# Second norm's last row block: the residual written into the accumulator banks, and the statistics read from them

## The chip, the cores and the metric

The kernel runs on one core of a Trainium2 chip. The engines named here are TensorE (PE in the profile, with its weight loads as PEld), VectorE (DVE), ScalarE (ACT), GpSimd (POOL) and SyncE (SP, which issues transfers). TensorE's results land in accumulator memory (PSUM); the kernel holds it as eight banks, each a tile of 128 partitions by 512 fp32 columns. The metric is device time in microseconds (us), the median of several executions; lower is better.

## The reference, cut to what matters

One decoder layer on 256 tokens of width 1024, batch 1. Only its last stage is touched:

```python
u = causal_dwconv(x @ w_up[l], conv_w_ffn[l])
f = (jax.nn.silu(u[..., :D_FF]) * u[..., D_FF:]) @ w_down[l]      # D_FF = 2816
x = layer_norm(DEEPNORM_ALPHA * x + f, ln2_g[l], ln2_b[l])        # over the 1024 columns
```

`layer_norm` takes mean and variance over the 1024 columns of a token, subtracts the mean, multiplies by 1/sqrt(variance + 1e-5) and by `ln2_g`, and adds `ln2_b`.

## The kernel before

Every fp32 operand of a product is split into a high and a low part (`h`, `l`), and each product is three matmuls (`mm3`: high by high, high by low, low by high), all added up in one bank. ScalarE makes the high parts of the weights (L196), VectorE the low ones (L205). The order of the work on each engine is written out by hand: an engine runs its instructions in the order in which the program issues them, and waits only where data or a buffer is not there. Those waits are put in from what each instruction reads and writes.

The down projection has 22 blocks (`NP`) of 128 rows of `w_down`. Its outputs are two row blocks of 128 tokens (`t` = 0 and 1) by two column halves (`nh`), in four banks: `dacc[t][nh]`. Blocks 0 to 13 go into all four banks inside the loop over the up projection's columns. The last eight blocks (`TAIL` = 8, blocks 14 to 21) go in a hand-written tail:

- L1012 to L1014: the eight blocks' products for row block 0, beside the last splits and the last pieces of the activation.
- L1029 to L1040: row block 0's norm on VectorE: `residual` (L797, and `bn_stats` in L799), `norm_stats` (`bn_aggr` in L781, the power -0.5 on GpSimd in L782), `norm_apply` (L786, L787) and two output transfers on SP's queue.
- Row block 1, on TensorE in this order: columns 0 to 511 of the eight blocks into `dacc[1][0]` (L1047), columns 512 to 767 into a fresh bank (e2, L1056), columns 768 to 1023 into another fresh bank (e3, L1062).
- Row block 1 on VectorE: the residual and what blocks 0 to 13 left in the banks are put into three SBUF pieces `part` (L1050), with their row sums. e2 is added to its piece (L1057). e3 is added last (L1076).

Row block 1's mean is known before its last columns are. ScalarE sums the `w_down` rows of blocks 14 to 21 over columns 768 to 1023 beside splitting them (`rowsum`, L199), scales the activations by these sums (`fs`, L1021), GpSimd adds the eight up (L1024), and TensorE multiplies the total by ones (`mean`, L1065): the sum over the last 256 columns of products that are not there yet. With the mean (L1068), ScalarE squares and sums the first 768 columns (L1071), VectorE subtracts the mean and multiplies by `ln2_g` (L1073, L1074), and behind the last bank VectorE adds it (L1076), squares and sums it (L1077), GpSimd takes the power -0.5 (L1079), and VectorE finishes in two pieces of 640 and 384 columns (L1082), each with its output transfer (L1083), the first on SP's queue and the second on ScalarE's.

Of the kernel before, what the change touches and what calls it, by code (L numbers as in the profile page):

```python
# [8 lines left out]
F32 = mybir.dt.float32  # L9
F32R = mybir.dt.float32r  # L10
BF16 = mybir.dt.bfloat16
I32 = mybir.dt.int32
AF = mybir.ActivationFunctionType
ALU = mybir.AluOpType

P = 128
S = 256
D = 1024
# [6 lines left out]
NP = DFF // P  # L25
ALPHA = 2.0 ** 0.25
EPS = 1e-5
# [22 lines left out]
CHUNK = 2048  # L50

PIECES = {0: (0, 768, 1280, 1792), 1: (0, 768, 1792)}
OFF_B, OFF_C, OFF_H, OFF_G = 3 * AW, 3 * AW + CW, 3 * AW + 2 * CW, 3 * AW + 3 * CW
TAIL = 8


def plan():
# [49 lines left out]
    for c in range(1, NP // 2):  # L107
# [4 lines left out]
        d = c - 1  # L112
        if 0 <= 2 * d < NP - TAIL:
            mark(("dn", d))
            rows("w_dn", 2 * d)
    for d in range((NP - TAIL) // 2, NP // 2):
        if ("dn", d) not in first:
# [20 lines left out]
def layer_kernel(ctx: ExitStack, tc: tile.TileContext, x, wpack, cpack, ln1_g, ln1_b, ln2_g, ln2_b, out):  # L138
    nc = tc.nc

    cst = ctx.enter_context(tc.tile_pool(name="cst", bufs=1))
    big = ctx.enter_context(tc.tile_pool(name="big", bufs=1))
    wp = ctx.enter_context(tc.tile_pool(name="wp", bufs=1))
    tmp = ctx.enter_context(tc.tile_pool(name="tmp", bufs=1))
# [11 lines left out]
    def scratch(shape, name, bufs=None, tag="scr"):  # L156
        return tmp.tile(shape, F32, tag=tag, name=name, bufs=bufs or 6)
# [4 lines left out]
    RAW_BUFS, HL_BUFS = 3, 9  # L162
    chunks, plan_units, U = plan()
# [13 lines left out]
                nc.sync.dma_start(xr, x[0].rearrange("(t p) d -> p t d", p=P))  # L177


    LAST_UNITS = [U[("dn", i // 2)] + i % 2 for i in range(NP - TAIL, NP)]  # L180
    rowsum = cst.tile([P, TAIL], F32, name="rowsum")

    def alloc(u, part, tag):
        k, n = units[u]["shape"]
# [7 lines left out]
    def split_h(u):  # L192

        issue_dma(units[u]["chunk"] + RAW_BUFS - 1)
        alloc(u, "h", "wh")
        nc.scalar.activation(units[u]["h"], raw_of(u), AF.Copy)  # L196
        if u in LAST_UNITS:
            j = LAST_UNITS.index(u)
            nc.scalar.activation(scratch([P, 256], f"rowsum{j}", tag="gs", bufs=3), raw_of(u)[:, 0, 768:1024], AF.Copy,  # L199
                                 accum_out=rowsum[:, j:j + 1])  # L200

    def split_l(u):

# [3 lines left out]
    def raw_of(u):  # L207
        un = units[u]
        k, n = un["shape"]
        return raws[un["chunk"]][:, un["off"]:un["off"] + k * n].rearrange("p (k n) -> p k n", k=k)  # L210
# [15 lines left out]
    def hl_split(h, l, src, eng=None):  # L226
        nc.scalar.activation(h, src, AF.Copy)  # L227
        (eng or nc.vector).tensor_tensor(l, src, h.bitcast(F32), op=ALU.subtract)  # L228
# [24 lines left out]
    neghalf = cst.tile([P, 1], F32, name="neghalf")  # L253
# [15 lines left out]
    xT = big.tile([P, KT, 2, S], F32R, tag="xT", name="xT")  # L269
# [43 lines left out]
    def mm3(o, ah, al, bh, bl, start, stop):  # L313

        nc.tensor.matmul(o, ah, bh, start=start, stop=False)  # L315
        nc.tensor.matmul(o, ah, bl, start=False, stop=False)  # L316
        nc.tensor.matmul(o, al, bh, start=False, stop=stop)  # L317
# [376 lines left out]
    for j in reversed(range(16)):  # L694
        u = U[("g", 0)] + j
# [26 lines left out]
    def ps_pair(name):  # L722
        return pairs.tile([P, 2, 512], F32, tag="pair", name=name)
# [65 lines left out]
    x1 = big.tile([P, 2, D], F32, tag="rows", name="x1")  # L789
    x1T = big.tile([P, KT, 2, S], F32R, tag="xT", name="x1T")  # L790

    def with_eps(stats):

        nc.vector.tensor_scalar(stats[:, 0, 2:3], stats[:, 0, 2:3], EPS * D, None, op0=ALU.add)
# [47 lines left out]
    ln2 = big.tile([P, 2, D], F32, tag="e8", name="ln2")  # L842
# [6 lines left out]
    def f_tile(i):  # L849
        g = i // 8  # L850
        if g not in FT:
            FT[g] = big.tile([P, 8, 2, S], F32R, tag=("b16", "c16", "b16")[g], name=f"f{g}")
        return FT[g][:, i % 8]
# [78 lines left out]
    dacc = [[acc_bank(f"d{t}{nh}") for nh in range(2)] for t in range(2)]  # L932

    def down(i, ts=(0, 1), nhs=(0, 1)):
        un = units[U[("dn", i // 2)] + i % 2]
        ft = f_tile(i)
        for t in ts:
            for nh in nhs:
                mm3(dacc[t][nh], ft[:, 0, t * P:(t + 1) * P], ft[:, 1, t * P:(t + 1) * P],
                    un["h"][:, 0, nh * 512:(nh + 1) * 512], un["l"][:, 0, nh * 512:(nh + 1) * 512],  # L940
                    i == 0, i == NP - 1 or (t == 1 and nh == 1 and i == NP - TAIL - 1))

    def down_part(i, bank, c):
        un = units[U[("dn", i // 2)] + i % 2]
        ft = f_tile(i)
        mm3(bank[:, 0:256], ft[:, 0, P:2 * P], ft[:, 1, P:2 * P],
            un["h"][:, 0, c * 256:(c + 1) * 256], un["l"][:, 0, c * 256:(c + 1) * 256], i == NP - TAIL, i == NP - 1)


    pending = []  # L950
# [11 lines left out]
    for c in range(1, NP // 2):  # L962
        for e in range(2):
            i = 2 * c + e
# [24 lines left out]
    for k, (kind, i, u) in enumerate(seq[:tail_from]):  # L989
        if kind == "g":  # L990
            pair, first_unit = ps_pair(f"pb{i}"), u
# [24 lines left out]

    fs = big.tile([P, TAIL, 2, P], F32, tag="d8", name="fs")
    for j in range(TAIL):  # L1020
        nc.scalar.activation(fs[:, j], f_tile(NP - TAIL + j)[:, :, P:2 * P].bitcast(F32), AF.Copy, scale=rowsum[:, j:j + 1])  # L1021

    def fs_add(a, b):
        nc.gpsimd.tensor_tensor(a, a, b, op=ALU.add)  # L1024

    fs_add(fs[:, 0:2], fs[:, 4:6])
    fs_add(fs[:, 2:4], fs[:, 6:8])

    r0 = x1[:, 0]  # L1029
    stats = tmp.tile([P, 4, 6], F32, tag="stats", name="rstats", bufs=2)  # L1030
    for nh in range(2):
        residual(0, nh, dacc[0][nh], x1, r0, stats, nh, nh * 512, nh * 512 + 512)
    mv = norm_stats(r0, stats, 2)
    fs_add(fs[:, 0:2], fs[:, 2:4])
    fs_add(fs[:, 0], fs[:, 1])
    fs_add(fs[:, 0, 0], fs[:, 0, 1])
    for c in range(2):
        cc = slice(c * 512, (c + 1) * 512)
        norm_apply(r0[:, cc], r0[:, cc], mv, ln2[:, 0, cc], ln2[:, 1, cc])
        nc.sync.dma_start(out[0, 0:P, cc], r0[:, cc])  # L1040


    cols3 = (slice(0, 512), slice(512, 768), slice(768, D))
    part = [scratch([P, cc.stop - cc.start], f"part{c}") for c, cc in enumerate(cols3)]
    sums = tmp.tile([P, 12], F32, tag="sums", name="sums", bufs=1)
    for i in range(NP - TAIL, NP):
        down(i, (1,), (0,))  # L1047
    for c in (1, 2, 0):
        bank = dacc[1][1][:, 256 * c - 256:256 * c] if c else dacc[1][0]
        nc.vector.scalar_tensor_tensor(part[c], x1[:, 1, cols3[c]], ALPHA, bank, op0=ALU.mult, op1=ALU.add,  # L1050
                                       accum_out=None if c == 1 else sums[:, c:c + 1])
    fsr = big.tile([P, 2, P], F32R, tag="xT", name="fsr")
    hl_split(fsr[:, 0], fsr[:, 1], fs[:, 0, 0])
    bank = ps_pair("e2")[:, 0]
    for i in range(NP - TAIL, NP):
        down_part(i, bank, 2)  # L1056
    nc.vector.scalar_tensor_tensor(part[1], bank[:, 0:256], 1.0, part[1], op0=ALU.mult, op1=ALU.add, accum_out=sums[:, 1:2])  # L1057
    nc.vector.tensor_reduce(sums[:, 3:4], sums[:, 0:3], axis=mybir.AxisListType.X, op=ALU.add)
    bank = ps_pair("e3")[:, 0]
    mean = acc_bank("mean")  # L1060
    for i in range(NP - TAIL, NP):
        down_part(i, bank, 3)  # L1062
        if i == NP - TAIL + 1:
            for part_hl in range(2):
                nc.tensor.matmul(mean[:, 0:2], fsr[:, part_hl], ones, start=part_hl == 0, stop=part_hl == 1)  # L1065

    for c, f in ((4, -1.0 / D), (5, -1.0 / (32 * D))):
        nc.vector.tensor_scalar(sums[:, c:c + 1], mean[:, 0:1], sums[:, 3:4], f, op0=ALU.add, op1=ALU.mult)  # L1068
    res = wp.tile([P, CHUNK], F32, tag="raw", name="res", bufs=RAW_BUFS)
    for c in range(2):  # L1070
        nc.scalar.activation(scratch([P, 512], f"sq{c}")[:, 0:cols3[c].stop - cols3[c].start], part[c], AF.Square,  # L1071
                             bias=sums[:, 5:6], scale=1.0 / 32, accum_out=sums[:, 6 + c:7 + c])
        nc.vector.scalar_tensor_tensor(res[:, cols3[c]], part[c], sums[:, 4:5], ln2[:, 0, cols3[c]], op0=ALU.add, op1=ALU.mult)  # L1073
    nc.vector.tensor_scalar(part[2], part[2], sums[:, 4:5], None, op0=ALU.add)  # L1074
    nc.vector.tensor_scalar(sums[:, 8:9], sums[:, 6:7], sums[:, 7:8], EPS, op0=ALU.add, op1=ALU.add)
    nc.vector.tensor_tensor(part[2], part[2], bank[:, 0:256], op=ALU.add)  # L1076
    nc.vector.tensor_tensor_reduce(out=scratch([P, 256], "sq2"), in0=part[2], in1=part[2], scale=1.0 / D, scalar=sums[:, 8:9],  # L1077
                                   op0=ALU.mult, op1=ALU.add, accum_out=sums[:, 9:10])
    nc.gpsimd.tensor_tensor(sums[:, 10:11], sums[:, 9:10], neghalf, op=ALU.pow)  # L1079
    nc.vector.scalar_tensor_tensor(res[:, cols3[2]], part[2], 1.0, ln2[:, 0, cols3[2]], op0=ALU.mult, op1=ALU.mult)  # L1080
    for cc, queue in ((slice(0, 640), nc.sync), (slice(640, D), nc.scalar)):
        nc.vector.scalar_tensor_tensor(res[:, cc], res[:, cc], sums[:, 10:11], ln2[:, 1, cc], op0=ALU.mult, op1=ALU.add)  # L1082
        queue.dma_start(out[0, P:2 * P, cc], res[:, cc])  # L1083


# [40 lines left out]
```

## Time and profile before

| what | value |
|---|---|
| median of 3 runs | 363.85 us (363.8 to 364.34) |
| the profiled execution | 364.61 us, of which the span shown by the profile is 362.8 us |
| mean granted TensorE clock | 0.995 |
| PE, PEld busy | 355.3 us, 307.0 us |
| DVE, ACT, POOL busy | 299.9 us, 235.4 us, 24.9 us |

The profile is of one execution. The "span" runs from its first to its last instruction. A timeline row gives the start from the beginning of the span, the duration, the engine, the line of the kernel, the operation, the tile it writes and those it reads, the count, and in brackets the idle time before it with whoever ended that. A group row gives the count, the total busy time, the mean in ns, and the idle time before. TensorE's matmuls overlap, so the distance between two starts, and not the duration, is what one matmul costs.

### The profile page before, as it was taken

To read this page: it belongs to the slowest core of one execution; us is meant where nothing else is said; L and a number is where in the kernel's file an instruction comes from. 1 tells how busy PE (TensorE), PEld (TensorE's weight loads), DVE (VectorE), ACT (ScalarE), POOL (GpSimd) and SP (SyncE) were. 2 spreads that over 40 slices of the span, in tenths; PEclk is the share of its full clock that TensorE was granted. 3 is DMA by queue.
4 is the path that set the end of the run, shared out by engine and by line. 5 is a ranking of instruction groups with operands and counts; after the bars stand their busy time and mean duration, and the time that the engine had idled before them with its cause. 6 is when DMAs were issued, how large, how long until landed. Compare 5 with 4: busy or idle time off the path is not lost.

```text
span 362.8 us, 5271 instructions
## 1 busy us (share of the span) xinstructions
PE 355.3 (98%) x1947; PEld 307.0 (85%) x1947; DVE 299.9 (83%) x518; ACT 235.4 (65%) x431; POOL 24.9 (7%) x48
## 2 busy tenths in 40 slices
PE   8999999999999999999999999999999999999993
PEld 7788888888898888888888888888888888888882
DVE  3787887989795979989769798978869696999795
ACT  4567858787977966653357566675757566588901
POOL 2000001000000113301000000000000000000060
PEclk9999999999999999999999999999999999999998
DMA  7978763626653354687160835447182745653011
GB/s 267 322 267 310 249 225 118 223 116 206 259 191 148 137 221 126 247 323 285 65 233 26 317 122 233 153 194 298 59 341 64 284 129 219 231 234 116 3 58 58
DMA packets 11099, 69.63 MB, mean 192 GB/s; under 512 B 1217, under 2 KB 1473, under 8 KB 4033
## 3 DMA queue, kind: packets, MB, share of 16 engines
q1 hardware_dynamic: 10352, 67.00, 50.4%
q0 software_dynamic: 576, 2.10, 1.7%
q8 instruction: 15, 0.25, 0.3%
q10 hardware_dynamic: 144, 0.20, 0.1%
q14 instruction: 12, 0.09, 0.1%
HBM read 68.24 MB, written 1.05 MB: 191 GB/s over the span
## 4 chain that ended last, share of the span: by engine, by line
PE 92%; issue 2%; DMA 2%; DVE 1%; POOL 1%; SPq 0%; ACT 0%; POOLq 0%; DVEq 0%
PE pb L333 20%; PE pb L340 11%; PE g L333 8%; PE d L315 4%; PE d L316 4%; PE d L317 4%; PE g L340 4%; PE y L333 4%; PE q L591 3%; PE v L591 3%; PE k L591 3%; PE b L333 2%; PE y L340 2%; PE c L333 2%; PE h L333 2%; PE o L316 2%
## 5 line engine op out<-in xcount | busy, mean ns | idle before, releaser
L205 DVE TENSOR_TENSOR wl<-raw,wh 128x1024 fp32r<-128x1024 f32 x99 | 122.1, 1235 | 23.3 <-ACT wh L196 22.7
L196 ACT ACTIVATE wh<-raw 128x1024 fp32r<-128x1024 f32 x99 | 103.7, 1054 | 26.9 <-DMA raw<-in_wpack 26.7
L333 PE MATMUL pb<-x1T,wh 128*128 128x512 f32 x320 | 76.2, 390 | 0.0
L333 PEld LDWEIGHTS pb<-x1T,wh 128*128 128x128 f32 x320 | 59.7, 188 | 12.1
L340 PEld LDWEIGHTS pb<-x1T,wl 128*128 128x128 f32 x320 | 41.0, 191 | 1.6
L340 PE MATMUL pb<-x1T,wl 128*128 128x256 f32 x320 | 41.5, 283 | 0.0
L228 DVE TENSOR_TENSOR wl<-raw,wh 128x1024 fp32r<-128x1024 f32 (+1 forms) x29 | 27.3, 982 | 7.2 <-ACT wh L227 7.0
L333 PE MATMUL g<-xT,wh 128*128 128x512 f32 x128 | 31.8, 395 | 0.0
L315 PE MATMUL d<-wh,f 128*128 128x512 f32 x80 | 31.3, 391 | 0.0
L316 PE MATMUL d<-wl,f 128*128 128x512 f32 x80 | 31.3, 391 | 0.0
L317 PE MATMUL d<-wh,f 128*128 128x512 f32 x80 | 31.1, 389 | 0.0
L227 ACT ACTIVATE wh<-raw 128x1024 fp32r<-128x1024 f32 (+1 forms) x29 | 23.7, 859 | 9.0 <-DMA raw<-in_wpack 5.1
L333 PEld LDWEIGHTS g<-xT,wh 128*128 128x128 f32 x128 | 23.2, 188 | 4.6
L858 ACT ACTIVATE fb<-pb 128x512 f32<-128x512 f32 x20 | 11.9, 596 | 16.8 <-PE pb L340 16.8
L876 DVE SCALAR_TENSOR_TENSOR fc<-fb,consts,fc 128x254 f32<-128x254 f32 x40 | 19.4, 484 | 1.4
L874 DVE SCALAR_TENSOR_TENSOR fc<-fb,consts,fc 128x255 f32<-128x255 f32 x40 | 19.1, 478 | 0.0
L868 ACT ACTIVATE fc<-fb,consts 128x256 f32<-128x256 f32 x40 | 18.0, 497 | 0.4 <-DVE fb L862 0.4
L317 PEld LDWEIGHTS d<-wh,f 128*128 128x128 f32 x80 | 15.0, 188 | 3.2
L1024 POOL TENSOR_TENSOR fs<-fs 128x512 f32<-128x512 f32 (+2 forms) x5 | 5.8, 1163 | 169.7 <-ACT fs L1021 169.5
L315 PEld LDWEIGHTS d<-wh,f 128*128 128x128 f32 x80 | 15.1, 189 | 2.7
L316 PEld LDWEIGHTS d<-wl,f 128*128 128x128 f32 x80 | 15.1, 189 | 2.6
L340 PEld LDWEIGHTS g<-xT,wl 128*128 128x128 f32 x128 | 16.4, 191 | 0.7
(207 smaller groups left out, 613.4 us busy)
## 6 DMA issues: line engine op xcount, KB each, us to landing
raw<-in_wpack SPq DMA_DIRECT2D x55, 1024.0 KB, 5.0
raw<-in_wpack SPq DMA_DIRECT2D x6, 896.0 KB, 6.8
xr<-in_x SPq DMA_DIRECT2D x1, 1024.0 KB, 7.0
ln<-in_ln_g POOLq DMA_DIRECT2D x2, 512.0 KB, 5.5
ln<-in_ln_b POOLq DMA_DIRECT2D x2, 512.0 KB, 6.1
raw<-in_wpack SPq DMA_DIRECT2D x2, 384.0 KB, 4.5
raw<-in_wpack SPq DMA_DIRECT2D x2, 256.0 KB, 4.3
raw<-in_wpack SPq DMA_DIRECT2D x1, 512.0 KB, 6.9
```

What stands on the lines that cost most here:

```text
L196: nc.scalar.activation(units[u]["h"], raw_of(u), AF.Copy)
L205: nc.vector.tensor_tensor(units[u]["l"], raw_of(u), units[u]["h"].bitcast(F32), op=ALU.subtract)
L227: nc.scalar.activation(h, src, AF.Copy)
L228: (eng or nc.vector).tensor_tensor(l, src, h.bitcast(F32), op=ALU.subtract)
L315: nc.tensor.matmul(o, ah, bh, start=start, stop=False)
L316: nc.tensor.matmul(o, ah, bl, start=False, stop=False)
L317: nc.tensor.matmul(o, al, bh, start=False, stop=stop)
L333: nc.tensor.matmul(bank, un["h"][:, k, n0:n0 + P], b[:, k].rearrange("p a s -> p (a s)"), start=k == 0, stop=False)
L340: nc.tensor.matmul(bank[:, 0:S], un["l"][:, k, n0:n0 + P], b[:, k, 0], start=False, stop=k == nk - 1)
L591: nc.tensor.matmul(banks[m][t], (xl if p == 2 else xh)[:, k, t * P:(t + 1) * P], wl if p == 1 else wh, start=k == 0 and p == 0, stop=k == ...
L874: nc.vector.scalar_tensor_tensor(c[:, 1:S], pb[:, a * S:a * S + S - 1], w_ffn(1, j), c[:, 1:S], op0=ALU.mult, op1=ALU.add)
L876: nc.vector.scalar_tensor_tensor(c[:, 2:S], pb[:, a * S:a * S + S - 2], w_ffn(0, j), c[:, 2:S], op0=ALU.mult, op1=ALU.add)
```

## The change

Row block 1's tail is written anew. `LAST` = 4 is the number of blocks for which the later columns are still open.

- The `rowsum` of ScalarE is taken for the last 4 blocks only, over columns 512 to 1023, and written to a tile of its own (`unread`).
- VectorE adds the residual into the banks: `seed` reads a bank, adds ALPHA times x1 and writes the result into a bank. `seed(0)` does it in place in `dacc[1][0]` (512 columns); `seed(1)` and `seed(2)` read the halves of `dacc[1][1]` and write each into a bank of one pair tile, `e`, with the row sums.
- TensorE's order for row block 1 becomes: blocks 14 to 17 by columns 512 to 1023 into `dacc[1][1]` (128x512 matmuls); blocks 14 to 21 by columns 0 to 511 onto the seeded `dacc[1][0]`; blocks 18 to 21 by columns 512 to 767 onto the first bank of `e`; and by columns 768 to 1023 onto the second (128x256 matmuls).
- ScalarE's `fs` and GpSimd's additions cover 4 blocks in place of 8, and all three additions stand ahead of row block 0's power on GpSimd.
- The copies `part`, the squares on ScalarE and VectorE and the three instructions with them are gone. `bn_stats` reads four pieces of 256 columns from the banks, `bn_aggr` joins the first two for the mean and all four for the variance, and `scaled` subtracts the mean and multiplies by `ln2_g`, straight from a bank.

```diff
-    LAST_UNITS = [U[("dn", i // 2)] + i % 2 for i in range(NP - TAIL, NP)]
-    rowsum = cst.tile([P, TAIL], F32, name="rowsum")
+    LAST_UNITS = [U[("dn", i // 2)] + i % 2 for i in range(NP - LAST, NP)]
+    rowsum = cst.tile([P, LAST], F32, name="rowsum")
+    unread = []
...
-            nc.scalar.activation(scratch([P, 256], f"rowsum{j}", tag="gs", bufs=3), raw_of(u)[:, 0, 768:1024], AF.Copy,
-                                 accum_out=rowsum[:, j:j + 1])
+            if j == 0:
+                unread.append(big.tile([P, LAST, 512], F32, tag="x", name="unread"))
+            nc.scalar.activation(unread[0][:, j], raw_of(u)[:, 0, 512:D], AF.Copy, accum_out=rowsum[:, j:j + 1])
...
-    def down_part(i, bank, c):
+    def down_on(i, bank, c0, c1):
         un = units[U[("dn", i // 2)] + i % 2]
         ft = f_tile(i)
-        mm3(bank[:, 0:256], ft[:, 0, P:2 * P], ft[:, 1, P:2 * P],
-            un["h"][:, 0, c * 256:(c + 1) * 256], un["l"][:, 0, c * 256:(c + 1) * 256], i == NP - TAIL, i == NP - 1)
+        for a, w in ((0, "h"), (0, "l"), (1, "h")):
+            nc.tensor.matmul(bank, ft[:, a, P:2 * P], un[w][:, 0, c0:c1], start=False, stop=a == 1 and i == NP - 1,
+                             skip_group_check=True)
...
+    sums = tmp.tile([P, 8], F32, tag="sums", name="sums", bufs=1)
+    def seed(c, o, bank, cc):
+        nc.vector.scalar_tensor_tensor(o, x1[:, 1, cc], ALPHA, bank, op0=ALU.mult, op1=ALU.add,
+                                       accum_out=sums[:, c:c + 1] if c else None)
+    cols3 = (slice(0, 512), slice(512, 768), slice(768, D))
+    seed(0, dacc[1][0], dacc[1][0], cols3[0])
+    for i in range(NP - TAIL, NP - LAST):
+        down(i, (1,), (1,))
+    pair = ps_pair("e")
+    tail_banks = (dacc[1][0], pair[:, 0, 0:256], pair[:, 1, 0:256])
+    fs = big.tile([P, LAST, 2, P], F32, tag="d8", name="fs")
+    for j in range(LAST):
+        nc.scalar.activation(fs[:, j], f_tile(NP - LAST + j)[:, :, P:2 * P].bitcast(F32), AF.Copy, scale=rowsum[:, j:j + 1])
...
-    fs_add(fs[:, 0:2], fs[:, 4:6])
-    fs_add(fs[:, 2:4], fs[:, 6:8])
+    fs_add(fs[:, 0:2], fs[:, 2:4])
+    fs_add(fs[:, 0], fs[:, 1])
+    fs_add(fs[:, 0, 0], fs[:, 0, 1])
+    fsr = big.tile([P, 2, P], F32R, tag="xT", name="fsr")
...
     mv = norm_stats(r0, stats, 2)
-    fs_add(fs[:, 0:2], fs[:, 2:4])
-    fs_add(fs[:, 0], fs[:, 1])
-    fs_add(fs[:, 0, 0], fs[:, 0, 1])
+    for c in (1, 2):
+        seed(c, tail_banks[c], dacc[1][1][:, 256 * c - 256:256 * c], cols3[c])
+    hl_split(fsr[:, 0], fsr[:, 1], fs[:, 0, 0])
+    nc.vector.tensor_tensor(sums[:, 3:4], sums[:, 1:2], sums[:, 2:3], op=ALU.add)
     for c in range(2):
...
         nc.sync.dma_start(out[0, 0:P, cc], r0[:, cc])
...
     mean = acc_bank("mean")
     for i in range(NP - TAIL, NP):
-        down_part(i, bank, 3)
-        if i == NP - TAIL + 1:
+        down_on(i, tail_banks[0], 0, 512)
+        if i == NP - 2:
             for part_hl in range(2):
                 nc.tensor.matmul(mean[:, 0:2], fsr[:, part_hl], ones, start=part_hl == 0, stop=part_hl == 1)
+    for c in (1, 2):
+        for i in range(NP - LAST, NP):
+            down_on(i, tail_banks[c], cols3[c].start, cols3[c].stop)
+    nc.vector.tensor_scalar(sums[:, 5:6], mean[:, 0:1], sums[:, 3:4], -1.0 / D, op0=ALU.add, op1=ALU.mult)
...
+    def scaled(c):
+        nc.vector.scalar_tensor_tensor(res[:, cols3[c]], tail_banks[c], sums[:, 4:5], ln2[:, 0, cols3[c]],
+                                       op0=ALU.add, op1=ALU.mult)
+    for piece, bank in enumerate((tail_banks[0][:, 0:256], tail_banks[0][:, 256:512], *tail_banks[1:])):
+        nc.vector.bn_stats(stats[:, piece, :], bank)
+        if piece == 1:
+            nc.vector.bn_aggr(mv[:, 0:2], stats[:, 0:2, :])
+            nc.vector.tensor_scalar(sums[:, 4:5], mv[:, 0:1], -512.0 / D, sums[:, 5:6], op0=ALU.mult, op1=ALU.add)
+            with_eps(stats)
+        if piece in (1, 2):
+            scaled(piece - 1)
+    nc.vector.bn_aggr(mv[:, 0:2], stats)
+    nc.gpsimd.tensor_tensor(mv[:, 3:4], mv[:, 1:2], neghalf, op=ALU.pow)
+    scaled(2)
     for cc, queue in ((slice(0, 640), nc.sync), (slice(640, D), nc.scalar)):
-        nc.vector.scalar_tensor_tensor(res[:, cc], res[:, cc], sums[:, 10:11], ln2[:, 1, cc], op0=ALU.mult, op1=ALU.add)
+        nc.vector.scalar_tensor_tensor(res[:, cc], res[:, cc], mv[:, 3:4], ln2[:, 1, cc], op0=ALU.mult, op1=ALU.add)
         queue.dma_start(out[0, P:2 * P, cc], res[:, cc])
```

The removed lines that are not shown are L1043 to L1058 and L1067 to L1080 of the kernel above.

More of the change, by code (lines that the diff above doesn't have):

```diff
@@ L54 @@
 TAIL = 8
+LAST = 4
 def plan():
@@ L940, in down @@
                     un["h"][:, 0, nh * 512:(nh + 1) * 512], un["l"][:, 0, nh * 512:(nh + 1) * 512],
-                    i == 0, i == NP - 1 or (t == 1 and nh == 1 and i == NP - TAIL - 1))
-    def down_part(i, bank, c):
+                    i == 0, i == (NP - 1 if t == 0 else NP - LAST - 1 if nh else NP - TAIL - 1))
+    def down_on(i, bank, c0, c1):
         un = units[U[("dn", i // 2)] + i % 2]
         ft = f_tile(i)
-        mm3(bank[:, 0:256], ft[:, 0, P:2 * P], ft[:, 1, P:2 * P],
-            un["h"][:, 0, c * 256:(c + 1) * 256], un["l"][:, 0, c * 256:(c + 1) * 256], i == NP - TAIL, i == NP - 1)
+        for a, w in ((0, "h"), (0, "l"), (1, "h")):
+            nc.tensor.matmul(bank, ft[:, a, P:2 * P], un[w][:, 0, c0:c1], start=False, stop=a == 1 and i == NP - 1,
+                             skip_group_check=True)
     pending = []
@@ L1015, in layer_kernel @@
     assert not pending
-    fs = big.tile([P, TAIL, 2, P], F32, tag="d8", name="fs")
-    for j in range(TAIL):
-        nc.scalar.activation(fs[:, j], f_tile(NP - TAIL + j)[:, :, P:2 * P].bitcast(F32), AF.Copy, scale=rowsum[:, j:j + 1])
+    sums = tmp.tile([P, 8], F32, tag="sums", name="sums", bufs=1)
[11 more added lines that the diff above has]
+        nc.scalar.activation(fs[:, j], f_tile(NP - LAST + j)[:, :, P:2 * P].bitcast(F32), AF.Copy, scale=rowsum[:, j:j + 1])
     def fs_add(a, b):
         nc.gpsimd.tensor_tensor(a, a, b, op=ALU.add)
-    fs_add(fs[:, 0:2], fs[:, 4:6])
-    fs_add(fs[:, 2:4], fs[:, 6:8])
+    fs_add(fs[:, 0:2], fs[:, 2:4])
+    fs_add(fs[:, 0], fs[:, 1])
+    fs_add(fs[:, 0, 0], fs[:, 0, 1])
+    fsr = big.tile([P, 2, P], F32R, tag="xT", name="fsr")
     r0 = x1[:, 0]
@@ L1040, in layer_kernel @@
         nc.sync.dma_start(out[0, 0:P, cc], r0[:, cc])
[L1043 to L1059, printed above, removed]
     mean = acc_bank("mean")
     for i in range(NP - TAIL, NP):
-        down_part(i, bank, 3)
-        if i == NP - TAIL + 1:
+        down_on(i, tail_banks[0], 0, 512)
@@ L1064, in layer_kernel @@
+        if i == NP - 2:
             for part_hl in range(2):
                 nc.tensor.matmul(mean[:, 0:2], fsr[:, part_hl], ones, start=part_hl == 0, stop=part_hl == 1)
-    for c, f in ((4, -1.0 / D), (5, -1.0 / (32 * D))):
-        nc.vector.tensor_scalar(sums[:, c:c + 1], mean[:, 0:1], sums[:, 3:4], f, op0=ALU.add, op1=ALU.mult)
+    for c in (1, 2):
+        for i in range(NP - LAST, NP):
+            down_on(i, tail_banks[c], cols3[c].start, cols3[c].stop)
+    nc.vector.tensor_scalar(sums[:, 5:6], mean[:, 0:1], sums[:, 3:4], -1.0 / D, op0=ALU.add, op1=ALU.mult)
@@ L1069, in layer_kernel @@
     res = wp.tile([P, CHUNK], F32, tag="raw", name="res", bufs=RAW_BUFS)
[L1070 to L1080, printed above, removed]
+    stats = tmp.tile([P, 4, 6], F32, tag="stats", name="rstats1", bufs=2)
@@ new lines, in layer_kernel @@
+    mv = tmp.tile([P, 4], F32, tag="mv", name="mv", bufs=4)
+    def scaled(c):
[9 more added lines that the diff above has]
+            scaled(piece - 1)
```

## The prediction

> **What bounds the kernel now.** I read the busy shares first, then the chain of waits, then each engine's timeline from 340 us on.
>
> ```profile
> span 362.8 us, 5271 instructions
> ...
> PE 355.3 (98%) x1947; PEld 307.0 (85%) x1947; DVE 299.9 (83%) x518; ACT 235.4 (65%) x431; POOL 24.9 (7%) x48
> ...
> PE 92%; issue 2%; DMA 2%; DVE 1%; POOL 1%; SPq 0%; ACT 0%; POOLq 0%; DVEq 0%
> ...
> 333.00:344.50 11.50, 11.50 (x57) 9.68 (x56) 9.32 (x16) 10.17 (x26) 0.57 (x1) 1.00 0.01 2
> ```
>
> TensorE has work for 355.3 of 362.8 us, and in the stretch ahead of the edit (333 to 344.5 us) it is busy all 11.50 us. So nothing that the edit does ahead of 344.9 us can start row block 1's products earlier; the time can come only from how long they take and from what follows the last of them. The products of row block 1:
>
> ```profile
> 344.00 0.39 PE L317 MATMUL d<-wh,f 128*128 128x512 f32 x1
> ...
> 344.91 0.39 PE L315 MATMUL d<-wh,f 128*128 128x512 f32 x1
> ...
> 350.35 0.28 PE L315 MATMUL e<-wh,f 128*128 128x256 f32 x1
> 350.46 0.28 PE L316 MATMUL e<-wl,f 128*128 128x256 f32 x1
> ...
> 353.82 0.28 PE L317 MATMUL e<-wh,f 128*128 128x256 f32 x1
> 353.94 0.28 PE L1065 MATMUL mean<-ones,fsr 128*128 128x2 f32 x2
> ...
> 354.29 0.28 PE L316 MATMUL e<-wl,f 128*128 128x256 f32 x1
> ...
> 356.21 0.28 PE L317 MATMUL e<-wh,f 128*128 128x256 f32 x1
> ```
>
> 24 matmuls of 512 columns take 350.35 - 344.91 = 5.44 us, 0.2267 each. 28 steps of 256 columns take 353.82 - 350.46 = 3.36 us, 0.120 each: more than half of a wide one. The two for the mean add 354.29 - 353.82 - 2 x 0.12 = 0.23 us. Then the end:
>
> ```profile
> 356.53 0.42 DVE L1076 TENSOR_TENSOR part<-part,e 128x256 f32<-128x256 f32 x1 [0.33 <-PE e L317]
> 356.98 0.48 DVE L1077 CUSTOM_DVE_ANT_0 sq<-part,sums 128x256 f32<-128x256 f32 x1
> 357.39 0.08 DVE L1077 DVE_READ_ACCUMULATOR2_ANT sums<- 128x1 f32 x1
> ...
> 357.55 0.66 POOL L1079 TENSOR_TENSOR sums<-sums,neghalf 128x1 f32<-128x1 f32 x1 [5.97 <-DVE sums L1077]
> ...
> 358.25 1.42 DVE L1082 SCALAR_TENSOR_TENSOR res<-res,sums,ln 128x640 f32<-128x640 f32 x2 [0.44 <-POOL sums L1079]
> ...
> 359.17 0.33 SPq L1083 DMA_DIRECT2D out<-res  x1
> ```
>
> VectorE idled 0.33 us for the last bank and started 0.32 us after the last matmul's start (356.53 - 356.21). From there: add, square, accumulator, 1.02 us to GpSimd (357.55), 0.70 us to VectorE's last pair (358.25), 4.55 us to the end of the span. The change leaves that last part alone.
>
> **The change part by part.**
>
> *TensorE's order.* The columns are the same, but 12 matmuls of 512 replace 24 of 256: 36 x 0.2267 + 24 x 0.12 + 0.23 = 11.27 us from 344.91, against 24 x 0.2267 + 48 x 0.12 + 0.23 = 11.43. The last start moves from 356.21 to 356.06: **-0.15 us**. Bounds: nothing, if each change of bank costs a small gap, and -0.31 if the 24 narrow ones left ran at half a wide step. The rows give the middle.
>
> *The end behind the last product.* Now a `bn_stats` of 256 columns from the bank, a `bn_aggr` of four pieces, then the power.
>
> ```profile
> L799 DVE BATCH_NORM_STATS2 rstats<-x 128x6 f32<-128x512 f32 x2 | 1.4, 694 | 0.1
> ...
> L1050 DVE SCALAR_TENSOR_TENSOR part<-x,d 128x256 f32<-128x256 f32 x2 | 0.7, 408 | 0.0
> ...
> L1050 DVE SCALAR_TENSOR_TENSOR part<-x,d 128x512 f32<-128x512 f32 x1 | 0.7, 678 | 0.0
> ...
> L1080 DVE SCALAR_TENSOR_TENSOR res<-part,ln 128x256 f32<-128x256 f32 x1 | 0.4, 422 | 0.0
> ...
> L1074 DVE TENSOR_SCALAR part<-part,sums 128x256 f32<-128x256 f32 x1 | 0.3, 349 | 0.0
> ...
> L781 DVE BATCH_NORM_AGGREGATE mv<-rstats 128x2 f32<-128x12 f32 x1 | 0.2, 211 | 0.0
> ...
> L794 DVE TENSOR_SCALAR rstats<-rstats 128x1 f32<-128x1 f32 x1 | 0.2, 153 | 0.0
> ```
>
> No row shows `bn_stats` on 256 columns or on a bank. Bounds: 0.694 (the 512-column row; half the columns can't cost more) and 0.349 (the cheapest 256-column row). From 512 to 256 columns L1050 falls by 0.27 us; I take 0.694 - 0.27 = 0.43. `bn_aggr` of four pieces lies between 0.153 (a one-element row) and 0.42 (twice the two-piece row); I take 0.22, as twelve elements more are little beside 0.211. With gaps of 0.02 and, to GpSimd, 0.08 (357.55 less 357.47, the accumulator's end), the power starts 0.43 + 0.02 + 0.22 + 0.08 = 0.75 us after VectorE's start, where it was 1.02: **-0.27 us**.
>
> Reading banks costs nothing extra by the rows: L1050, with the bank as an operand, takes 0.408 and L1080, all in SBUF, 0.422. [...]
>
> *The power itself.* L1079 took 0.663 us; its twin on the `mv` tile, which the change uses, took less:
>
> ```profile
> L782 POOL TENSOR_TENSOR mv<-mv,neghalf x3: 550/556/561, 162.9 to 347.7; 128x1 f32<-128x1 f32 x3
> ```
>
> The one stands at the same place, the other is the same instruction; I take 0.61, **-0.05 us**, with 0 and -0.11 as ends. `scaled(2)` runs under it, as L1080 did.
>
> *Is VectorE there in time?* Bank 0's last product starts at 344.91 + 35 x 0.2267 + 0.23 = 353.07. In the trace the row at 344.00 closes the bank that VectorE takes up at 344.43, so bank 0 is readable at 353.50; the last bank at 356.06 + 0.32 = 356.38. Between them stand six steps and the mean's small ones.
>
> ```profile
> 352.05 0.74 DVE L1050 SCALAR_TENSOR_TENSOR part<-x,d 128x256 f32<-128x256 f32 x2
> ...
> 354.26 0.34 DVE L1068 TENSOR_SCALAR sums<-mean,sums 128x1 f32<-128x1 f32 x2
> 354.52 1.14 DVE L1073 SCALAR_TENSOR_TENSOR res<-part,sums,ln 128x512 f32<-128x512 f32 x2
> ...
> L1073 DVE SCALAR_TENSOR_TENSOR res<-part,sums,ln 128x512 f32<-128x512 f32 x1 | 0.7, 746 | 0.0
> ...
> L1073 DVE SCALAR_TENSOR_TENSOR res<-part,sums,ln 128x256 f32<-128x256 f32 x1 | 0.5, 480 | 0.0
> ```
>
> Instructions that don't depend on each other overlap: L1050's two take 0.74, a step of 0.33; L1073's two take 1.14, so the second starts 0.66 after the first. Two pieces 0.33 + 0.43, `bn_aggr` 0.23, the mean 0.24 (0.21 and a gap), epsilon's step 0.1, `scaled(0)` 0.66, the third piece 0.35, `scaled(1)` 0.48: 2.82 us of 2.88. VectorE is just there, with 0.06 us to spare: the forecast's weak point.
>
> *What is hidden.*
>
> ```profile
> 342.05 0.42 DVE L892 TENSOR_TENSOR f<-ff,f 128x256 fp32r<-128x256 f32 x1
> 344.43 0.69 DVE L797 SCALAR_TENSOR_TENSOR x<-x,d 128x512 f32<-128x512 f32 x1 [1.96 <-PE d L317]
> ...
> 347.39 0.21 DVE L781 BATCH_NORM_AGGREGATE mv<-rstats 128x2 f32<-128x12 f32 x1
> 347.64 0.78 DVE L786 SCALAR_TENSOR_TENSOR x<-x,mv,ln 128x512 f32<-128x512 f32 x1
> 348.52 1.60 DVE L787 SCALAR_TENSOR_TENSOR x<-x,mv,ln 128x512 f32<-128x512 f32 x1
> 350.04 1.22 DVE L786 SCALAR_TENSOR_TENSOR x<-x,mv,ln 128x512 f32<-128x512 f32 x1
> ...
> 341.36 3.30 ACT L1021 ACTIVATE fs<-f,rowsum 128x256 f32<-128x256 f32 x8
> ...
> 343.93 2.55 POOL L1024 TENSOR_TENSOR fs<-fs 128x512 f32<-128x512 f32 x2 [169.53 <-ACT fs L1021]
> ...
> 348.20 3.38 POOL L1024 TENSOR_TENSOR fs<-fs 128x512 f32<-128x512 f32 x3
> ```
>
> `seed(0)` (0.68) fits VectorE's idle 1.96 us from 342.47; TensorE needs it at 344.91 + 12 x 0.2267 = 347.63. `seed(1)` and `seed(2)` wait for `dacc[1][1]`, last start 347.40 and readable at 347.83, where VectorE is free at 347.60: the queue behind them (the split of `fsr`, a sum, row block 0's `norm_apply` and its two output transfers) starts about 1.4 us later than L786 did. But GpSimd's additions are over by then: half of L1021's rows from 341.36 (the last waits for block 21's low part, 342.47), then one addition of each size, 343 to about 346.3. L787 took 1.60 and L786 1.22 us beside them, against 0.78 without, so four at 0.75 end near 352.1, as before. Row block 0's transfers issue about when they did. The mean's scalar is there after 352.8; VectorE waits for bank 0 with 1.4 us to spare. A seed's write into a bank, shown by no row, would have to cost 1.4 us more to matter. The mean's products (TensorE, after 352.4) need `fsr`, done by 349. Banks 1 and 2 need their seeds at 353.30, done by 348.7. On ScalarE eight 256-column sums become four of 512 columns; if they ran late, a split's high part would stop TensorE, but they are fewer and start four blocks later. Each of these is costed at nothing.
>
> Sum: -0.15 - 0.27 - 0.05 = **-0.47 us**, in the profiled execution 364.61 to 364.14; that one lies 0.76 us above the median, so I carry the difference over: 363.85 - 0.47 = 363.38 us.
>
> **The rivals.**
>
> *VectorE late (B).* Every piece at 0.694 would put it 3 x 0.27 - 0.06 = 0.75 us behind the last bank and cost 0.27 at the end: -0.47 + 1.02 = +0.55, 364.4. Against it: rows of half the columns fall by 0.27. A smaller case: forms of one width differ by 0.07 (L1073's 0.480 on 256 columns beside L1050's 0.408); each of the six reads from banks so much dearer than I take it makes 5 x 0.07 - 0.06 + 0.07 = +0.36, 363.74. [...]
>
> *A wait that reaches too far (C), slower than before.* The third piece reads the pair tile's first bank while TensorE still writes its second. If the wait is put in by tile and not by bank, that piece waits for the last product (356.38), and piece, `scaled(1)`, piece, `bn_aggr` follow: 0.35 + 0.42 + 0.43 + 0.24 + 0.08, the power at 357.90 for 357.55. That is +0.35, less 0.05 for the power: 364.15; with both late pieces at 0.694, +0.84, 364.7. Against it: GpSimd's first addition started at 343.93, after six of the eight L1021 (341.36 + 6 x 0.41 = 343.8) and ahead of the eighth's end at 344.66, so waits follow parts of an SBUF tile; for a bank pair no row tells.
>
> *A larger gain (D).* Pieces at 0.349, `bn_aggr` at 0.153, the power at 0.55 and narrow matmuls at half a step: -0.31 - 0.42 - 0.11 = -0.84, 363.0. Several floors at once would be needed.
>
> **How the numbers follow.** Forecast 56%, B 12%, C 16%, D 16%. The predicted time is 363.4. The range reaches down to D and up to B and C without dear pieces, 363.0 to 364.4. Within 0.2% (0.73 us, about what a measurement of this kernel can tell from no change) lie 363.12 to 364.58. Faster: two thirds of D (0.11) and 0.16 of the forecast's 0.56, as the three runs lie 0.54 us apart: 0.27. Slower: half of C with dear pieces (0.09), B with a further delay (0.04), the forecast 0.02: 0.15. No change: 0.58.
>
> **What would show it.** In the profile of the changed kernel: row block 1's products on TensorE without a gap from 344.9 to a last start near 356.06; `bn_stats` on 256 columns at 0.43; VectorE idle, however shortly, ahead of the fourth piece with TensorE as its releaser (if it is busy there, B; if the third piece waits for the last product, C); the power starting near 357.1; L787's successors at 0.75. A gap at a change of bank, or a `scaled` well above 0.75, would make it wrong.

## The result: slower by 0.16%, and the profile after

| kernel | median | runs | ratio to before, 95% interval |
|---|---|---|---|
| before | 364.27 us (363.45 to 364.88) | 22 | |
| changed | 364.72 us (364.13 to 365.25) | 22 | 1.0016 [1.0009, 1.0022] |

The interval makes it 0.3 to 0.8 us slower, 0.58 by the ratio. The kernel before also measured 0.42 us higher over 22 runs than over the three that the prediction had.

The profiled execution of the changed kernel took 364.13 us, the fastest of its 22, with a span of 362.4 us: shorter than the 362.8 before. Read as a whole the two profiles would say "faster". The span is made up of three stretches (up to row block 1's first product, from there to VectorE's last pair, and from there to the end), and only the first differs by luck.

TensorE's timeline of the changed kernel: row block 1's first product, the first and the last of 256 columns.

```profile
343.83 0.39 PE L319 MATMUL d<-wh,f 128*128 128x512 f32 x1
...
352.23 0.28 PE L952 MATMUL e<-wh,f 128*128 128x256 f32 x1
...
354.98 0.28 PE L952 MATMUL e<-wh,f 128*128 128x256 f32 x1
```

Row block 1's products start at 343.83 here and at 344.91 before: this execution was 1.08 us ahead when it came to row block 1. That is not the change's doing: the six other profiles with the new order of products, below, have this start between 344.02 and 345.56, and a second profile of the kernel before has it at 344.01. From the first product to the last is 354.98 - 343.83 = 11.15 us, as forecast. What VectorE and GpSimd do behind it, in their timelines:

```profile
352.43 0.76 DVE L1085 BATCH_NORM_STATS2 rstats<-d 128x6 f32<-128x256 f32 x2 [0.58 <-PE d L952]
...
353.72 0.75 DVE L1081 SCALAR_TENSOR_TENSOR res<-d,sums,ln 128x512 f32<-128x512 f32 x1
355.30 0.43 DVE L1085 BATCH_NORM_STATS2 rstats<-e 128x6 f32<-128x256 f32 x1 [0.83 <-PE e L952]
355.64 0.47 DVE L1081 SCALAR_TENSOR_TENSOR res<-e,sums,ln 128x256 f32<-128x256 f32 x1
356.03 0.42 DVE L1085 BATCH_NORM_STATS2 rstats<-e 128x6 f32<-128x256 f32 x1
356.48 0.26 DVE L1093 BATCH_NORM_AGGREGATE mv<-rstats 128x2 f32<-128x24 f32 x1
...
356.83 0.55 POOL L1094 TENSOR_TENSOR mv<-mv,neghalf 128x1 f32<-128x1 f32 x1 [9.70 <-DVE mv L1093]
...
357.41 1.41 DVE L1097 SCALAR_TENSOR_TENSOR res<-res,mv,ln 128x640 f32<-128x640 f32 x2 [0.33 <-POOL mv L1094]
```

The first bank of the pair gets its own last product about 1.4 us ahead of the last product of all. By the forecast the third piece follows `scaled(0)` (L1081, at 353.72) without a gap, some 0.6 us ahead of that last product. Instead VectorE stands idle for 0.83 us and starts the third piece at 355.30, 0.32 us after the *last* matmul's start; the fourth piece follows without any idle time. From row block 1's first product to VectorE's last pair it is 357.41 - 343.83 = 13.58 us, where it was 358.25 - 344.91 = 13.34: +0.24 in place of -0.47.

The third stretch, from VectorE's last pair to the end, was 362.81 - 358.25 = 4.56 us and is 362.37 - 357.41 = 4.96 (the spans to two places). The program's closing line is where it grows: there all engines wait for each other. The rows of that line (instruction, count, durations in ns, first and last start in us), before and after:

```profile
L1122 POOLq EVENT_SEMAPHORE  x4: 17/17/17, 362.1 to 362.7; - x4
...
L1122 DVEq EVENT_SEMAPHORE  x2: 21/21/21, 362.2 to 362.8; - x2
```

```profile
L1137 POOLq EVENT_SEMAPHORE  x4: 17/17/17, 361.2 to 362.3; - x4
...
L1137 DVEq EVENT_SEMAPHORE  x2: 21/21/21, 361.7 to 362.3; - x2
```

GpSimd gathers the other engines with its first semaphore instruction and releases them with its second: in the records the first waits for a semaphore that the others count up, and the others wait for the one that the second sets, their next semaphore instructions starting 0.04 to 0.06 us after it in both profiles. VectorE's row shows the release. Before it came 0.1 us after the gathering, now 0.5. The records in full: GpSimd's first two semaphore instructions there start at 362.07 and 362.15 before, and at 361.22 and 361.66 after: 0.08 and 0.44 us, for instructions of 17 ns. Behind the second one the rows run as before, but for 0.05 us more in GpSimd's next instruction there (a drain of 148 ns in place of 102).

So two losses, neither in what the change computes: a wait of the third piece, and a stop of GpSimd in the closing barrier.

### The profile page after: what moved, and what is told of

It is laid out like the page before. It is cut to its first block, busy times and chain, and to the rows that moved or that the text cites. A ratio compares the mean times of both kernels' runs of the same rounds, so it can differ in the third digit from the quotient of the medians.

```text
span 362.4 us, 5224 instructions
## 1 busy us (share of the span) xinstructions
PE 354.2 (98%) x1935; PEld 306.0 (84%) x1935; DVE 298.0 (82%) x518; ACT 232.5 (64%) x415; POOL 21.5 (6%) x46
## 4 chain that ended last, share of the span: by engine, by line
PE 59%; DVE 17%; DMA 13%; issue 6%; ACT 3%; POOLq 0%; POOL 0%; DVEq 0%; ACTq 0%
DMA raw<-in_wpack 13%; PE g L337 8%; DVE wl L209 8%; PE pb L337 5%; PE g L344 4%; PE y L337 4%; PE q L595 3%; PE k L595 3%; PE v L595 3%; PE pb L344 3%; ACT wh L199 2%; DVE fc L878 2%; PE b L337 2%; PE y L344 2%; PE c L337 2%
## 5 line engine op out<-in xcount | busy, mean ns | idle before, releaser
L320 PE MATMUL d<-wl,f 128*128 128x512 f32 x76 | 29.8, 392 | 0.0
L319 PE MATMUL d<-wh,f 128*128 128x512 f32 x76 | 29.8, 392 | 0.0
L321 PE MATMUL d<-wh,f 128*128 128x512 f32 x76 | 29.7, 390 | 0.0
L321 PEld LDWEIGHTS d<-wh,f 128*128 128x128 f32 x76 | 14.3, 188 | 3.2
L344 PE MATMUL g<-xT,wl 128*128 128x256 f32 x128 | 16.6, 282 | 0.0
L320 PEld LDWEIGHTS d<-wl,f 128*128 128x128 f32 x76 | 14.3, 189 | 2.6 <-DVE wl L209 0.2
L319 PEld LDWEIGHTS d<-wh,f 128*128 128x128 f32 x76 | 14.3, 189 | 2.6
```

The source lines that it names most:

```text
L344: nc.tensor.matmul(bank[:, 0:S], un["l"][:, k, n0:n0 + P], b[:, k, 0], start=False, stop=k == nk - 1)
```

## The experiments

All are the changed kernel or the one before with a few lines edited, and none leaves a part of the computation out. The first four lines of the table are the two programs that each edit is compared with. "Tail" is from row block 1's first product to VectorE's last pair, "end" from there to the span's end, "gap" is between GpSimd's first two semaphore instructions in the closing barrier; all are starts in the trace of one execution. Each ratio is to the kernel before, measured beside it on the same chip; its median there was 364.27 us in the third line, 364.17 in the next three and 364.34 in the next three, so the ratios and not the medians are compared between these groups.

| kernel | first product at | tail | end | gap | median, us | ratio, 95% interval |
|---|---|---|---|---|---|---|
| before | 344.91 | 13.34 | 4.56 | 0.08 | 364.27 | |
| before, again | 344.01 | 13.34 | 4.56 | 0.08 | (one execution, 363.7) | |
| changed | 343.83 | 13.58 | 4.96 | 0.44 | 364.72 | 1.0016 [1.0009, 1.0022] |
| changed, again | 344.34 | 13.58 | 4.95 | 0.43 | 364.77 | 1.0020 [1.0011, 1.0030] |
| two tiles | 344.63 | 12.85 | 4.97 | 0.44 | 364.22 | 1.0003 [0.9994, 1.0011] |
| two tiles, wait by order | 344.02 | 13.58 | 4.94 | 0.43 | 364.81 | 1.0018 [1.0009, 1.0027] |
| two tiles, padded | 344.56 | 12.86 | 4.54 | 0.08 | 363.74 | 0.9987 [0.9979, 0.9996] |
| changed, padded | 345.56 | 13.58 | 4.55 | 0.08 | 364.39 | 1.0004 [0.9993, 1.0015] |
| before, shortened | 344.74 | 13.34 | 4.96 | 0.44 | 364.77 | 1.0013 [1.0004, 1.0022] |
| changed, one more | 344.57 | 13.58 | 4.74 | 0.08 | (one execution, 364.65) | |

**The changed kernel and the one before, again.**

> The changed kernel once more, for a second profile and a time beside the others on one chip. Theory C: 0.2 to 0.6 us above the kernel before, the stretch from row block 1's first product to VectorE's last pair again 13.55 to 13.6 us whatever happens ahead of it; the part behind VectorE's last pair (5.0 us in the first profile, 4.55 before) returns to within 0.1 us of 4.55 if that was chance, stays at 5.0 if the change causes it.

> The kernel before, for a second profile of it. The stretch from row block 1's first product to VectorE's last pair is again 13.3 to 13.4 us; the start of row block 1's first product moves by up to 1 us between executions, and the part behind VectorE's last pair is 4.5 to 4.6 us if it is the kernel's own.

Tail and end of each program repeat to 0.01 us, while the first product's start moves by 0.9 us between the two executions of the kernel before, and by 1.7 us over all ten, and decides how long a single execution is. The changed kernel's time was 0.60 us above the kernel before by the medians, the upper end of what was expected. The longer end is not chance: it is the changed program's own.

**The pair tile taken apart.**

```diff
-    pair = ps_pair("e")
-    tail_banks = (dacc[1][0], pair[:, 0, 0:256], pair[:, 1, 0:256])
+    tail_banks = (dacc[1][0], *[ps_pair(f"e{c}")[:, 0, 0:256] for c in (1, 2)])
```

> The two 256-column banks become two tiles in place of one pair tile; nothing else changes. Theory C (the third piece's wait is put in for the whole pair tile): VectorE's third piece starts when bank 1 is done, about 1.4 us ahead of the last product, the fourth piece starts 0.32 us after the last matmul's start, and the stretch from row block 1's first product to VectorE's last pair falls from 13.58 us to about 12.85; the time about 0.7 us below the changed kernel and 0.3 to 0.5 us below the one before. Rival (reading or seeding banks is dear, or the loss lies ahead of the tail or behind it): third piece earlier perhaps, but the time within 0.2 us of the changed kernel.

VectorE's timeline of the two-tile kernel; its last matmul starts at 355.77:

```profile
354.52 0.75 DVE L1080 SCALAR_TENSOR_TENSOR res<-d,sums,ln 128x512 f32<-128x512 f32 x1
355.18 0.42 DVE L1084 BATCH_NORM_STATS2 rstats<-e 128x6 f32<-128x256 f32 x1
355.52 0.47 DVE L1080 SCALAR_TENSOR_TENSOR res<-e,sums,ln 128x256 f32<-128x256 f32 x1
356.09 0.43 DVE L1084 BATCH_NORM_STATS2 rstats<-e 128x6 f32<-128x256 f32 x1
356.56 0.26 DVE L1092 BATCH_NORM_AGGREGATE mv<-rstats 128x2 f32<-128x24 f32 x1
...
357.48 1.41 DVE L1096 SCALAR_TENSOR_TENSOR res<-res,mv,ln 128x640 f32<-128x640 f32 x2 [0.33 <-POOL mv L1093]
```

The third piece now follows `scaled(0)` without a gap and 0.59 us ahead of the last product; the 1.4 us of the expectation left out that VectorE is busy with `scaled(0)` until then. The fourth starts 0.32 us after the last matmul's start, and 0.10 us lie between `scaled(1)`'s end (355.99) and it. The tail is 0.73 us shorter, 12.85. In the trace's records the changed kernel's third piece carries a wait for TensorE's semaphore and its fourth none, so the one wait covered all products into the tile; in the two-tile kernel each carries its own. The kernel before had a tile of its own for each of its two late banks (`e2`, `e3`). The time fell by 0.55 us (364.77 to 364.22, measured side by side), near the 0.7 expected, but only to that of the kernel before and not 0.3 to 0.5 us below it, since the end stayed at 4.97.

**The wait put back by the order of the pieces.**

```diff
-    for piece, bank in enumerate((tail_banks[0][:, 0:256], tail_banks[0][:, 256:512], *tail_banks[1:])):
+    for piece, bank in enumerate((tail_banks[0][:, 0:256], tail_banks[0][:, 256:512], tail_banks[2], tail_banks[1])):
...
-            scaled(piece - 1)
+            scaled(2 * (piece - 1))
...
-    scaled(2)
+    scaled(1)
```

> As the two-tile kernel, but VectorE reads the later bank first, so that its third piece waits for the last product again, now by the order of the data and not by a shared tile. Theory C: the 0.7 us come back, within 0.15 us of the changed kernel, the stretch again about 13.55 us. Rival (the pair tile costs in another way, in seeding or on TensorE): stays at the two-tile kernel's time.

VectorE's timeline of that kernel, whose last matmul starts at 355.16:

```profile
355.48 0.43 DVE L1084 BATCH_NORM_STATS2 rstats<-e 128x6 f32<-128x256 f32 x1 [0.83 <-PE e L952]
```

The same 0.83 us of idle time, the same tail of 13.58, and the changed kernel's time (364.81 beside 364.77). Two tiles are not faster in themselves; the gain comes from the early start of the third piece.

**GpSimd's program made as long as before.** The changed GpSimd program lacks two additions and one wait: the trace has 74 records of its instructions in place of 77. Three memsets that nobody reads make up for them; they stand at the start of the kernel (at 2.56 us), nearly 360 us ahead of the barrier.

```diff
         nc.gpsimd.memset(invf[:, i:i + 1], f)
+    pad = cst.tile([P, 3], F32, name="pad")
+    for i in range(3):
+        nc.gpsimd.memset(pad[:, i:i + 1], 0.0)
```

> The two-tile kernel with three one-column memsets more at GpSimd's start, on a tile that nobody reads; they only make GpSimd's program three instructions longer, as long as before the change. Theory F (the changed GpSimd program is three instructions shorter, so a block of its instructions is fetched in the closing barrier, where GpSimd stands still for 0.36 us): the 0.44 us between GpSimd's two semaphore instructions there fall to 0.08, the 8 KB instruction transfer at 361 us is gone from the end, the part behind VectorE's last pair is 4.55 us again, and the time is 0.3 to 0.45 us below the two-tile kernel, 0.3 to 0.5 us below the one before. Rival (the end is longer for another cause, the output transfers or the new last instructions): 4.9 to 5.0 us stay, and the time of the two-tile kernel.

> The changed kernel with the same three memsets. Theory F with theory C: the end returns to 4.55 us, the tail keeps its 13.55 us, and the time is 0.3 to 0.45 us below the changed kernel, 0.15 to 0.3 us above the one before: the two losses are separate and add. Rival: no change against the changed kernel.

The rows of the closing line in the padded two-tile kernel:

```profile
L1139 POOLq EVENT_SEMAPHORE  x4: 17/17/17, 361.2 to 361.9; - x4
...
L1139 DVEq EVENT_SEMAPHORE  x2: 21/21/21, 361.4 to 361.9; - x2
```

Both padded kernels have the short gap and the short end. The two-tile one is 0.48 us faster than without padding by the medians (364.22 to 363.74), 0.58 by the ratios, a little more than expected, and faster than the kernel before (0.13%, 0.04 to 0.21%). The changed one is 0.3 to 0.4 us faster than without by the medians, 0.4 to 0.6 by the ratios, and level with the kernel before, where 0.15 to 0.3 us above it was expected.

**The kernel before, made shorter.** Three of its eight `invf` memsets go to VectorE, nothing else.

```diff
-        nc.gpsimd.memset(invf[:, i:i + 1], f)
+        (nc.gpsimd if i < 5 else nc.vector).memset(invf[:, i:i + 1], f)
```

> The kernel before with three of the eight one-column memsets at its start moved from GpSimd to VectorE, so that GpSimd's program is three instructions shorter and all else the same. Theory F: the 8 KB instruction transfer and the 0.36 us stop appear in the closing barrier of the old kernel too, the part behind VectorE's last pair is 4.9 to 5.0 us in place of 4.55, and the time is 0.3 to 0.45 us above the kernel before. Rival: within 0.15 us of the kernel before, 4.55 us.

```profile
L1122 POOLq EVENT_SEMAPHORE  x4: 17/17/17, 361.9 to 362.9; - x4
...
L1122 DVEq EVENT_SEMAPHORE  x2: 21/21/21, 362.4 to 363.0; - x2
```

The old kernel, with its tail of 13.34 us untouched, gets the gap of 0.44 us, the end of 4.96 and 0.43 us on its median. VectorE's program is three instructions longer here, but in the padded kernels only GpSimd's differs. The loss belongs to the length of GpSimd's program and not to the change's arithmetic.

**One instruction more.** One memset in place of three, in the changed kernel, one execution.

```diff
+    pad = cst.tile([P, 1], F32, name="pad")
+    nc.gpsimd.memset(pad, 0.0)
```

> The changed kernel with one memset more on GpSimd. Theory F, with the block's end just between GpSimd's two semaphore instructions of the closing barrier: one instruction more moves the block's end ahead of the first of them, where GpSimd waits for the others anyway; the 8 KB transfer comes at about 358 us, behind the power, in place of 361.9, the gap in the barrier is 0.08 us and the part behind VectorE's last pair 4.55 us. Rival (any shorter program, or the count of work instructions, costs the 0.4 us): 4.95 us stay.

The gap is 0.08 as expected, so a single instruction is enough to take the stop out of the barrier. The end is 4.74 and not 4.55: the last outputs land 2.4 us after their issue and not 2.2. The transfers of the stretch from 359.4 to 361 us, while they land:

```profile
q14 instruction: 1, 0.01, 2.1%
```

One instruction transfer lies among them there, near 359.65 us and not at about 358 as expected. That it holds the outputs up by 0.2 us is likely and not shown. The total of a single execution tells nothing at this size.

## Why the prediction was wrong, step by step

- **TensorE's order, -0.15.** Right. First to last matmul start is 11.15 us in the changed kernel (11.30 before), without a gap at a change of bank: the steps across the three changes are 0.23, 0.23 and 0.12 us, no longer than other steps behind a matmul of the same width.
- **The end behind the last product, -0.27, and the power, -0.05.** Right where the fourth piece alone is behind the last product: in the two-tile kernel from 356.09 to 357.48 it is 1.39 us; forecast 0.75 + 0.61 + 0.04. A piece of 256 columns from a bank takes 0.43, as taken; `bn_aggr` of four 0.26 for 0.22; the power 0.55 for 0.61. The same instruction from a bank and from SBUF shows what the bank costs: `scaled` takes 0.75 us for 512 columns and 0.47 for 256 from a bank, where L1073 took 0.746 and 0.480 from SBUF: nothing beyond 0.01 us.
- **Is VectorE there in time?** The reckoning of the steps was right to 0.04 us (0.10 spare for 0.06 once the wait is gone), but it is the step that failed: it took for granted that the third piece needs its own bank alone. The wait for the whole pair put 0.83 us of idle time ahead of that piece and 0.73 us on the tail. The rival that was given 16%, the wait that reaches too far, is what happened, at the price worked out for it: from the third piece's start to the power 356.83 - 355.30 = 1.53 us, forecast 357.90 - 356.38 = 1.52. The evidence held against it, GpSimd's start after six of eight `fs` rows, was of an SBUF tile, and the wait here is on a pair of banks: what held for the one did not hold for the other.
- **"The change leaves that last part alone."** This second step failed too, and no rival had it. The end grew by 0.40 us, because GpSimd's program became three instructions shorter. The prediction priced what GpSimd does, and gave the number of its instructions no price.
- **What is hidden.** Right. The seeds, the later `norm_apply` and the sums cost nothing: TensorE has no gap, and VectorE waits ahead of bank 0 (0.58 us). VectorE's timeline of the changed kernel has 0.75 us for each step of `norm_apply`, where two of them took 1.60 and 1.22 us before:

```profile
348.74 0.75 DVE L791 SCALAR_TENSOR_TENSOR x<-x,mv,ln 128x512 f32<-128x512 f32 x1
349.41 0.75 DVE L790 SCALAR_TENSOR_TENSOR x<-x,mv,ln 128x512 f32<-128x512 f32 x1
350.19 0.75 DVE L791 SCALAR_TENSOR_TENSOR x<-x,mv,ln 128x512 f32<-128x512 f32 x1
...
351.63 0.22 DVE L1075 TENSOR_SCALAR sums<-mean,sums 128x1 f32<-128x1 f32 x1 [0.68 <-PE mean L1071]
```

Of the 1.34 us between the forecast 363.38 and the measured 364.72, 0.42 is the higher time of the kernel before and 0.92 the change, +0.45 on the medians in place of -0.47. The sum as it came out: 12.85 - 13.34 = -0.49 for the tail once the wait is gone (forecast -0.47), +0.73 for the wait, +0.40 for the longer end: +0.64 by the profiles, within the 0.3 to 0.8 us that the runs give. The forecast's range up to 364.4 covered the wait (C priced it at +0.30, the tail shows +0.24), but neither the longer end nor the 0.42 us by which three runs had put the kernel before too low. With both taken away the kernel is 0.13% faster than before, 0.47 us by the ratio, with an interval of 0.15 to 0.77; that this is the forecast's figure to the digit is chance.

## What to carry to other kernels

The tile that spans two banks was waited for as one here (0.83 us of idle time): where one bank is read while the other is still being written, give each its own tile, and look in the trace for a reader that starts with the last writer of the tile and not with its own. A gain or loss of a few tenths of a microsecond is not read from two spans: cut the executions at points that the edit can't move, and compare the stretches, which here repeat to 0.01 us while the spans of one kernel differ by 0.9. And when an edit changes how many instructions an engine has, compare the closing barrier in both profiles before the edit is judged.

## What the runs showed of the hardware that was not expected

GpSimd stood still for about 0.36 us (0.44 - 0.08) between two 17 ns instructions in the five executions whose GpSimd had 74 records, and not in the five with 75 or 77. The instruction transfers go with the number too: the four executions with 77 records have one on q14 between 174.7 and 178.2 us that the other six lack, and those six have one at their end (359.65 us in the one with 75 records, 362.4 to 363.3 in the five with 74). I had expected this transfer to be what GpSimd waits for, and it is not. In the changed kernel's transfers from 361 to 363 us (40 slices of 0.05 us, the digit the busy share in tenths) it is the only one,

```profile
DMA  0000000000000000000000000005000000000000
...
q14 instruction: 1, 0.01, 1.4%
```

and it lies near 362.35 us, 0.7 us after GpSimd went on at 361.66. So the stop goes with the length of the program. That a block of GpSimd's instructions ends there and another is fetched (theory F) was my estimate; no run shows it, and what the engine does in the stop stays open. In the page of the kernel before q14 has 12 instruction transfers (0.09 MB, about 8 KB each), and the other queue that carries such transfers, q8, has 15 (0.25 MB, some 16 KB each).
